# The first experts without two TensorE products, the branch for extra blocks two experts earlier, and y evicted before it is split

## The chip, the cores and the metric

The kernel is one program on one NeuronCore of a Trainium2 chip. Its five engines are TensorE (PE in the profile), VectorE (DVE), ScalarE (ACT), GpSimd (POOL) and SyncE (SP), which here only issues DMAs. The metric is the time of one execution on the device, in microseconds (us), as a median over runs.

## The reference

256 tokens of width 1024 go through a first block (retention, a feed-forward layer, stick-breaking attention, another feed-forward layer) and then through a second block. The change lies wholly in the second block's last part, a mixture of 32 experts in 4 groups: each token takes the best group, and in it the best two experts. Cut to what matters:

```python
g_prob = softmax(xt @ w_rg + b_rg)
g_w, g_idx = top_k(g_prob, 1)                 # the group
e_top, e_loc = top_k(e_logits of that group, 2)
e_w = softmax(e_top) * g_w                    # two weights a token
# every expert e, for the tokens sent to it:
y = (silu(x @ w_gate[e]) * (x @ w_up[e])) @ w_down[e]     # 1024 -> 2 x 512 -> 1024
out[token] += y * e_w
...
x = x + gate2 * ffn                           # gate2: one row of 1024 numbers
return rms_norm(x, g_final)
```

`gate2` is the last of six rows that a small product of `c` with `w_ada` gives. There is no limit on how many tokens an expert takes.

## The kernel before, in words

**Weights.** All weights stream from HBM in loads of 1 MB through a ring of slots, in the order that `plan` writes down, all issued on SP (`Stream.fill`, L132). In the experts the order is four loads of gate and up weights of expert 0 (`gu`), four of expert 1, two of down weights of expert 0 (`dn`), four of expert 2, two of down weights of expert 1, and so on; the last are `gu` 31, `dn` 30, `dn` 31. Before the experts the ring is extended to 21 slots. A load is issued when PE has read the slot that it goes into, so up to 21 loads are ahead of PE.

**Routing.** `last` (L1484 on) ends the norm in front of the experts. For each half of the tokens (t = 0, 1) `choose` finds groups and experts on DVE, `rank` (PE, tile `next`) counts each token's place in its expert, and `first_hot` (DVE, tile `goh`) makes the one-hot matrix that picks the rows of experts 0 and 1. `gather_steps` multiplies it on PE with x (tile `xg`, L1715); `gather_out` brings the result to SBUF with scale and shift. Small `idle` products (L1417) keep PE going between. `position`, `weights` and `route_rest` finish the slots and weights of all tokens, `spread` makes `gate2` in 128 partitions on PE (tile `gate`, L650), and `spread_rows` does the same for positions and weights (tile `rows`, L1651).

**An expert.** An expert has 64 slots, and two experts a pair q = e // 2. `gate_up` is 16 matmuls of 512 columns (two records each in the trace: x32), L1736, then SiLU on ACT and a product on DVE. `h_T` transposes the result on PE (L1748) and DVE copies it (L1757). `down` is 8 matmuls (x16), L1771. `evac` brings each half of y out of PSUM, times weight and gate (DVE, L1888), and splits it into a high part `Yh` (ACT, L364) and a low part `Yl` (DVE, L365). `sc` (L1899) adds a pair's rows to the tokens' sums in PSUM (tile `acc`) by 8 matmuls with a matrix S of slots; the sums have begun with x, put there by 8 products with the identity (`add_x`, L1906). Every two pairs, `gather` (L1694) fetches the rows of the next ones, and `one_hot` makes its matrix on DVE.

**The order of the loop** is written out in `experts`. In turn e: `gate_up(e)`; for odd e, `sc` of the pair before and S of this pair; `dn(e - 1)`, with the transposition of e in its middle; at some e the gather. `overflow` holds the blocks of experts with more than 64 rows. It is a loop under a condition on a count, and every engine reads the count (L1812) and branches by itself (L1813); here the count is 0 and the body does not run. It stands at the end of turn 30, behind `dn(29)`, since it uses ring slots that are free only once all loads have been issued. After the last `sc` come the final norm and four output DMAs.

Of the kernel before, what the change touches and what calls it, by code (L numbers as in the profile page):

```python
# [12 lines left out]
F32 = mybir.dt.float32  # L13
# [8 lines left out]
T = 256  # L22
# [18 lines left out]
I2 = 2  # L41
# [153 lines left out]
class Body:  # L195
# [418 lines left out]
    def ada_steps(self):  # L614
        nc = self.nc
        for s in range(4):
            p = self.w("ada")
            for kc in range(KC):
# [5 lines left out]
                if kc == KC - 1:  # L624
# [3 lines left out]
                    if s == 1:  # L628

                        self.row1 = self.dram.tile([4 * 384], F32, name="row1")  # L630
                        nc.gpsimd.dma_start(out=self.row1.rearrange("(g c) -> g c", g=4), in_=m[0:128:32, :])
# [10 lines left out]

    def spread(self, s, t):

        nc = self.nc
        for i in range(2):
            r = self.w("gate")
            for j in range(4):
                k = 12 * s + 4 + 4 * i + j
                nc.tensor.matmul(r[:, j * 128:j * 128 + 128], self.modc[:, k:k + 1].to_broadcast([128, 128]), self.ident,  # L650
                                 start=True, stop=True)
            nc.scalar.activation(t[:, i * 512:i * 512 + 512], r, AF.Copy)
        return t
# [438 lines left out]
    def mixers(self, xT):  # L1092
# [281 lines left out]
        def gate(_):  # L1374
            self.gate = self.view("gain", [128, D], "gate")
            nc.sync.dma_start(out=self.gate, in_=self.row1[512:1536].partition_broadcast(128))
# [26 lines left out]
    def open_experts(self):  # L1403
# [6 lines left out]
        self.declare(mp, k2=2)  # L1410
        self.st.extend(mp, "ring2", RING2, RING2)
# [36 lines left out]
    def router_norm(self):  # L1448
# [33 lines left out]
        def last():  # L1482
# [29 lines left out]
    def choose(self, t, p, mid=None):  # L1512
# [7 lines left out]
        OH = [rt(f"oh{k}", NT, 32) for k in range(2)]  # L1520
# [21 lines left out]
        V.tensor_scalar(OH[1][:, t, :], io, ei[:, t, 1:2], None, op0=ALU.is_equal)  # L1542
# [11 lines left out]
    def first_hot(self, t, q):  # L1554

        V = self.nc.vector
# [6 lines left out]
    def position(self, t, q):  # L1563
# [3 lines left out]
        lim, tmp, pos = rt("lim", 32), rt("tmp", 32), rt("pos", NT, 2)  # L1567
        V.tensor_tensor(lim, q, self.rc["past"], op=ALU.is_ge)
# [16 lines left out]

    def route_rest(self):
# [5 lines left out]

        se, d, wt = rt("se"), rt("d"), rt("wt", NT, 2)
        V.scalar_tensor_tensor(se, d, 1.0, se, op0=ALU.add, op1=ALU.mult)
        V.reciprocal(wt[:, :, 0], se)
# [6 lines left out]
        for r, src in zip(self.rowsb, (pos, wt)):  # L1602
            yield
            self.spread_rows(r, src)
# [574 lines left out]
```

## Time and profile before

| | |
|---|---|
| three runs | 1367.05, 1364.13, 1362.34 us; median 1364.13 |
| the profiled execution | 1361.64 us, of which the span of its trace is 1359.6 us |
| PE busy | 1323.8 us, 97% of the span |
| DVE, ACT, POOL busy | 867.1, 631.2, 60.1 us |
| moved by DMA | 374.64 MB, at a mean of 276 GB/s |
| the experts | gather from 890.0, first `gate_up` from 896.9, end of the last `dn` 1345.8 us |

Times within the trace count from the span's start. A row of the timeline is a run of like instructions: its start, its length, engine, line, operation, and output and input tiles; in brackets at its end stands how long the engine had been idle before it and which instruction ended the wait. `PEq`, `DVEq` and `SPq` are the engines' sequencers, which hold branches and DMA issues.

### The profile page before, as it was taken

To read this page: it belongs to the slowest core of one execution; us is meant where nothing else is said; L and a number is where in the kernel's file an instruction comes from. 1 tells how busy PE (TensorE), PEld (TensorE's weight loads), DVE (VectorE), ACT (ScalarE), POOL (GpSimd) and SP (SyncE) were. 2 spreads that over 40 slices of the span, in tenths; PEclk is the share of its full clock that TensorE was granted. 3 is DMA by queue.
4 is the path that set the end of the run, shared out by engine and by line. 5 is a ranking of instruction groups with operands and counts; after the bars stand their busy time and mean duration, and the time that the engine had idled before them with its cause. 6 is when DMAs were issued, how large, how long until landed. Compare 5 with 4: busy or idle time off the path is not lost. (4 is left out here: it accounts for less than half of the span.)

```text
span 1359.6 us, 21183 instructions
## 1 busy us (share of the span) xinstructions
PE 1323.8 (97%) x8108; PEld 975.2 (72%) x8108; DVE 867.1 (64%) x1823; ACT 631.2 (46%) x1227; POOL 60.1 (4%) x117
## 2 busy tenths in 40 slices
PE   9999999999999999999999999999999999999986
PEld 7888878999989998999996899864434434344332
DVE  7757757777776666877777778645635544544344
ACT  5554546666667776666666666532212111111112
POOL 0000001000010000000002222100000000000000
PEclk9999999999999999999999999989999999999998
DMA  9755459544447323844446844789999999999994
GB/s 362 303 191 180 132 207 398 198 186 186 155 164 293 115 95 121 356 186 186 185 141 228 368 166 160 276 328 370 420 420 421 420 421 421 420 421 421 421 420 162
DMA packets 56857, 374.64 MB, mean 276 GB/s; under 512 B 7085, under 2 KB 7905, under 8 KB 15666
## 3 DMA queue, kind: packets, MB, share of 16 engines
q1 hardware_dynamic: 55440, 369.66, 69.2%
q0 software_dynamic: 1168, 3.54, 0.8%
q8 instruction: 64, 1.05, 0.3%
q14 instruction: 39, 0.32, 0.1%
q10 hardware_dynamic: 146, 0.07, 0.0%
HBM read 372.19 MB, written 1.05 MB: 275 GB/s over the span
## 5 line engine op out<-in xcount | busy, mean ns | idle before, releaser
L157 DVE TENSOR_TENSOR lo<-ring,hi 128x512 fp32r<-128x512 f32 x519 | 334.9, 687 | 100.5 <-ACT hi L154 94.6
L154 ACT ACTIVATE hi<-ring 128x512 fp32r<-128x512 f32 x519 | 300.6, 623 | 119.8 <-PE nat_ps L360 40.2
L1736 PE MATMUL gu<-ring,x 128*64 128x512 f32 x920 | 207.2, 598 | 15.9 <-DVEq L1813 5.6
L358 PE MATMUL up<-xT,hi 128*128 128x256 f32 x704 | 199.5, 283 | 0.0
L360 PE MATMUL up<-xT,lo 128*128 128x256 f32 x704 | 199.2, 283 | 0.0
L359 PE MATMUL up<-xT,hi 128*128 128x256 f32 x704 | 199.2, 283 | 0.0
L1736 PEld LDWEIGHTS gu<-ring,x 128*64 128x64 f32 x920 | 64.9, 138 | 147.9 <-issue 117.7
L364 ACT ACTIVATE Yh<-y 64x512 fp32r<-64x512 f32 x64 | 40.2, 629 | 213.8 <-DVE y L1888 182.3
L358 PEld LDWEIGHTS up<-xT,hi 128*128 128x128 f32 x704 | 134.0, 190 | 2.0 <-issue 1.2
L359 PEld LDWEIGHTS up<-xT,hi 128*128 128x128 f32 x704 | 134.0, 190 | 0.8
L360 PEld LDWEIGHTS up<-xT,lo 128*128 128x128 f32 x704 | 134.0, 190 | 0.0
L1771 PE MATMUL y<-ring,early 128*64 128x512 f32 x480 | 115.4, 602 | 1.2 <-DMA ring<-dn 0.6
L1740 ACT ACTIVATE h<-gu 64x512 f32<-64x512 f32 x32 | 18.8, 589 | 156.4 <-PE gu L1736 123.5
L813 DVE SCALAR_TENSOR_TENSOR slab<-up,conv,slab 128x254 f32<-128x254 f32 (+1 forms) x176 | 72.7, 476 | 25.7 <-ACT slab L809 25.2
L1741 DVE TENSOR_TENSOR h<-h,gu 64x512 f32<-64x512 f32 x32 | 22.1, 692 | 102.5 <-ACT h L1740 101.8
L365 DVE TENSOR_TENSOR Yl<-y,Yh 64x512 fp32r<-64x512 f32 x64 | 43.9, 686 | 45.7 <-ACT Yh L364 45.7
L358 PE MATMUL nat_ps<-hi,xT 128*128 128x512 f32 x176 | 69.2, 393 | 0.0
L360 PE MATMUL acc<-hi,slab 128*128 128x512 f32 x176 | 69.2, 393 | 0.0
L358 PE MATMUL acc<-hi,slab 128*128 128x512 f32 x176 | 68.9, 391 | 0.0
L359 PE MATMUL acc<-lo,slab 128*128 128x512 f32 x176 | 68.7, 390 | 0.0
L360 PE MATMUL nat_ps<-hi,xT 128*128 128x512 f32 x176 | 68.6, 390 | 0.0
L359 PE MATMUL nat_ps<-lo,xT 128*128 128x512 f32 x176 | 68.6, 390 | 0.0
(450 smaller groups left out, 2509.8 us busy)
## 6 DMA issues: line engine op xcount, KB each, us to landing
ring<-gu SPq DMA_DIRECT2D x123, 1024.0 KB, 19.8
ring<-dn SPq DMA_DIRECT2D x59, 1024.0 KB, 19.8
ring<-ffn_u SPq DMA_DIRECT2D x44, 1024.0 KB, 4.9
ring<-ada SPq DMA_DIRECT2D x32, 768.0 KB, 4.3
ring<-ret_w SPq DMA_DIRECT2D x22, 1024.0 KB, 11.1
ring<-ffn_d SPq DMA_DIRECT2D x22, 1024.0 KB, 4.9
ring<-sb SPq DMA_DIRECT2D x12, 1024.0 KB, 6.3
ring<-ret_o SPq DMA_DIRECT2D x8, 1024.0 KB, 9.2
```

Source lines behind the costliest of these rows:

```text
L154: self.nc.scalar.activation(hi, src, AF.Copy)
L157: (eng or self.nc.vector).tensor_tensor(lo, src, hi.bitcast(F32), op=ALU.subtract)
L358: mm(out, l[0], r[0], start=start, stop=False, **k)
L359: mm(out, l[0], r[1], start=False, stop=False, **k)
L360: mm(out, l[1], r[0], start=False, stop=stop, **k)
L364: self.nc.scalar.activation(hi, src, AF.Copy)
L365: self.nc.vector.tensor_tensor(lo, src, hi.bitcast(F32), op=ALU.subtract)
L813: nc.vector.scalar_tensor_tensor(u[:, c, s:], p[:, c * T:c * T + T - s], cw[:, n - 1 - s:n - s], u[:, c, s:], op0=ALU.mult, op1=ALU.add)
L1736: nc.tensor.matmul(p[64 * i:64 * i + 64, :], xs(kc), raw[:, i * 512:i * 512 + 512], start=kc == 0, stop=kc == KC - 1)
L1740: nc.scalar.activation(h[64:128, :], p[0:64, :], AF.Silu)
L1741: nc.vector.tensor_tensor(h[64:128, :], h[64:128, :], p[64:128, :], op=ALU.mult)
L1771: nc.tensor.matmul(p[64 * i:64 * i + 64, :], hT[:, c, :], raw[:, h * 512:h * 512 + 512], start=c == 0, stop=c == 3)
```

## The change

It has three parts.

- **The first experts.** `gate2` is no longer made on PE. Its row is written to HBM by a DMA on POOL's queue and read back into 128 partitions by a second one, where the ring is extended (512 KB). The sums begin with copies of x into PSUM by ACT (three) and DVE (one), in `seed`, so `add_x` goes. Both `spread_rows` come before expert 1's `gate_up`, not behind it. The first one-hot matrix is made on POOL, the first gather is four steps of four matmuls with the second `rank` behind the first, and no idle products stand between.
- **The branch** (`overflow`) moves from the end of turn 30 to turn 29, behind `gate_up(29)`, `sc(13)`, the load of the final norm's gain and the transposition of 29; that result goes into the free half of the gain's ring slot. `dn(28)` and the gather that stood ahead of it are now behind it.
- **y.** Both halves are evicted, then both are split. `sc` multiplies all high parts first and then all low parts. Seven idle products stand ahead of the last `sc`.

The first place is PE at the start of the experts. Before, from the idle products behind the first `rank` to the first half of `dn(0)` (`next` is a rank, `gate` the spread of gate2, `acc<-x` the sums' beginning):

```order
L1417 MATMUL idle<-ident 128x128 x4
L1715 MATMUL xg<-goh,x 128x128 x8
L1548 MATMUL next<-early 128x32
L1550 MATMUL next<-M,early 128x32
L1551 MATMUL next<-M,early 128x32
L1417 MATMUL idle<-ident 128x128 x2
L1715 MATMUL xg<-goh,x 128x128 x8
L1736 MATMUL gu<-ring,xg 64x512 x16
L650 MATMUL gate<-ident,modc 128x128 x8
L1748 MATMUL hT<-ident,h 128x64 x4
L1906 MATMUL acc<-x,ident 128x512 x4
L1736 MATMUL gu<-ring,xg 64x512 x16
```

And now, over the same stretch up to expert 1's `gate_up`:

```order
L1409 MATMUL idle<-ident 128x128 x4
L1732 MATMUL xg<-goh,x 128x128 x4
L1551 MATMUL next<-early 128x32
L1553 MATMUL next<-M,early 128x32
L1554 MATMUL next<-M,early 128x32
L1732 MATMUL xg<-goh,x 128x128 x12
L1753 MATMUL gu<-ring,xg 64x512 x16
L1668 MATMUL rows<-ident,pos 128x128 x4
L1668 MATMUL rows<-ident,wt 128x128 x4
L1765 MATMUL hT<-ident,h 128x64 x4
L1753 MATMUL gu<-ring,xg 64x512 x16
```

The second `rank` stands four gather products earlier, the `gate` and `acc` products are gone, and the `rows` products, which followed expert 1's `gate_up`, stand ahead of it.

The second place is PE around the branch. Before, it stands behind `dn(29)`:

```order
L1736 MATMUL gu<-ring_12657,x 64x512 x4
L1771 MATMUL y<-ring_12663,early 64x512 x4
L1748 MATMUL hT<-ident,h 128x64 x4
L1771 MATMUL y<-ring,early 64x512 x4
L1812 TENSOR_LOAD tabi
L1813 COMPARE_AND_BRANCH
```

And now behind the transposition of 29, with `dn(28)` still to come:

```order
L1753 MATMUL gu<-ring,x 64x512 x16
L1922 MATMUL acc<-Yh,S 128x512 x4
L1922 MATMUL acc<-Yl,S 128x512 x4
L1765 MATMUL hT<-ident,h 128x64 x4
L1828 TENSOR_LOAD tabi
L1829 COMPARE_AND_BRANCH
```

What PE had done ahead of the branch, `dn(28)`, a gather, `gate_up(30)` and `dn(29)`, now follows it.

The third place is DVE at the end, from the copy of the last transposition on (`y` is the product with weight and gate, `Yl` the low part). Before:

```order
L1757 COPY early<-hT 128x256
L1888 SCALAR_TENSOR_TENSOR y<-y,ws,gate_10392 64x512
L365 TENSOR_TENSOR Yl<-y,Yh 64x512
L1888 SCALAR_TENSOR_TENSOR y<-y,ws,gate_10392 64x512
L365 TENSOR_TENSOR Yl<-y,Yh 64x512
L1888 SCALAR_TENSOR_TENSOR y<-y,ws,gate_10392 64x512
L365 TENSOR_TENSOR Yl<-y,Yh 64x512
```

And now:

```order
L1774 COPY early<-hT 128x256
L1907 SCALAR_TENSOR_TENSOR y<-y,ws,gate_10117 64x512 x2
L367 TENSOR_TENSOR Yl<-y,Yh 64x512 x2
L1907 SCALAR_TENSOR_TENSOR y<-y,ws,gate_10117 64x512 x2
L367 TENSOR_TENSOR Yl<-y,Yh 64x512 x2
```

The product of the second half no longer stands behind the low part of the first.

The diff, cut to its core:

```diff
-I2 = 2
+I2 = 7
+OVER = E - 3
...
-    def spread(self, s, t):                      # gate2 on PE: gone
...
     def open_experts(self):
...
+        self.gate2 = mp.tile([128, D], F32, name="gate2")
+        nc.gpsimd.dma_start(out=self.gate2, in_=self.gates[3][512:1536].partition_broadcast(128))
...
             self.idle(I1)
-            self.choose(1, p, lambda: self.first_hot(0, q0))
-            self.xg0 = self.gather_steps(self.first, 128)
-            next(self.xg0)
+            qs = self.small("q0")
+            nc.scalar.activation(qs, q0[:, 0:2], AF.Copy)
+            self.first_hot(0, qs, nc.gpsimd)
+            self.choose(1, p)
+            xg = self.gather_steps(self.first, 128)
+            next(xg)
             q1 = self.rank(1)
-            self.idle(I2)
+            next(xg)
             self.first_hot(1, q1)
-            self.qs = q0, q1
+            self.weights()
+            self.table("silu")
+            self.sums = [self.seed(0, (nc.scalar, nc.scalar))]
+            for t, q in enumerate((q0, q1)):
+                self.position(t, q)
+            next(xg)
+            self.xg0 = next(xg)
+            self.sums.append(self.seed(1, (nc.vector, nc.scalar)))
+            self.slot_weights()
+            self.split_x()
...
+    def seed(self, t, engs):
+        out = []
+        for h, eng in enumerate(engs):
+            p, x = self.a("acc"), self.x[:, t, h * 512:h * 512 + 512]
+            if eng is self.nc.scalar:
+                eng.activation(p, x, AF.Copy)
+            else:
+                eng.tensor_copy(p, x)
+            out.append(p)
+        return out
...
-        for i in (odd, 1 - odd):
-            r, h = slice(64 * i, 64 * i + 64), i ^ odd
-            evac(i, r, h, p[r, :])
+        rows = [slice(64 * i, 64 * i + 64) for i in (odd, 1 - odd)]
+        evac([(r, h, p[r, :]) for h, r in enumerate(rows)])
...
+            def evac(parts):
+                fs = []
+                for r, h, p in parts:
+                    f = mp.tile([128, 512], F32, tag="k2", name="y", bufs=2)
+                    nc.vector.scalar_tensor_tensor(f[r, :], p, W[e // 2][h][r, :], ...)
+                    fs.append(f)
+                for (r, h, _), f in zip(parts, fs):
+                    self.hilo(hi[r, h, :], lo[r, h, :], f[r, :])
...
-            if e > 1 and odd:
-                sc(q - 1)
+            if odd:
+                if e > 1:
+                    sc(q - 1)
+                if e == OVER:
+                    gain = st.spare()
+                    nc.sync.dma_start(out=gain[:, 0:D], in_=a["g_final"].partition_broadcast(128))
+                    hTs[e] = self.h_T(hs.pop(e), gain[:, D:D + 256].rearrange(...))()
+                    self.overflow(accs)
+                    hot(q + 1)
                 S[q] = slots(self.slot_rows, q)
...
-                dn(e - 1, turn)
...
+                dn(e - 1, turn if e in hs else None)
+            else:
+                self.all_rows()
                 turn()()
-                self.split_x()
-                add_x()
...
-            if e == E - 2:
-                gain = st.spare()
-                nc.sync.dma_start(out=gain[:, 0:D], in_=a["g_final"].partition_broadcast(128))
-                self.overflow(accs)
         dn(E - 1)
+        self.idle(I2)
         sc(E // 2 - 1)
```

## Rows read from the trace of the kernel before

**Rows 1.** Page, parts 1 and 2: busy time; GB/s in 40 slices.

```profile
PE 1323.8 (97%) x8108; PEld 975.2 (72%) x8108; DVE 867.1 (64%) x1823; ACT 631.2 (46%) x1227; POOL 60.1 (4%) x117
...
GB/s 362 303 191 180 132 207 398 198 186 186 155 164 293 115 95 121 356 186 186 185 141 228 368 166 160 276 328 370 420 420 421 420 421 421 420 421 421 421 420 162
```

**Rows 2.** Windows, core 0: engines' busy time, TensorE clock, DMA share, GB/s.

```profile
888.00:890.00 2.00, 2.00 (x10) 2.00 (x11) 1.72 (x11) 0.80 (x5) 0.41 (x2) 0.50 0.99 414
...
896.00:904.00 8.00, 8.00 (x42) 3.07 (x41) 2.83 (x16) 1.50 (x4) 0.00 (x0) 1.00 0.57 179
...
910.00:914.00 4.00, 4.00 (x21) 1.43 (x22) 2.54 (x11) 0.00 (x0) 0.00 (x0) 1.00 0.57 168
...
928.00:936.00 8.00, 7.57 (x36) 2.64 (x38) 1.74 (x4) 1.41 (x4) 0.00 (x0) 1.00 0.66 211
```

**Rows 3.** Timeline of PE from 884 to 931: start, length, group, wait.

```profile
890.02 3.39 PE L1715 MATMUL xg<-goh,x 128*128 128x128 f32 x16
...
894.94 2.05 PE L1715 MATMUL xg<-goh,x 128*128 128x128 f32 x16
...
896.92 7.09 PE L1736 MATMUL gu<-ring,xg 128*64 128x512 f32 x32
...
903.94 2.05 PE L650 MATMUL gate<-ident,modc 128*128 128x128 f32 x16
...
906.31 3.70 PE L1906 MATMUL acc<-x,ident 128*128 128x512 f32 x8
...
909.94 7.09 PE L1736 MATMUL gu<-ring,xg 128*64 128x512 f32 x32
...
916.96 1.16 PE L1651 MATMUL rows<-ident,pos 128*128 128x128 f32 x8
...
918.94 1.94 PE L1771 MATMUL y<-ring,early 128*64 128x512 f32 x8
...
928.43 1.94 PE L1736 MATMUL gu<-ring,x 128*64 128x512 f32 x8 [0.76 <-DVE x L1725]
```

**Rows 4.** Timeline of the SP queue, 895 to 935: weight loads issued.

```profile
898.90 0.33 SPq L132 DMA_DIRECT2D ring<-dn  x1
...
917.07 13.67 SPq L132 DMA_DIRECT2D ring<-gu  x4
```

**Rows 5.** Groups by shape on POOL: busy us, mean ns, idle before.

```profile
L1167 POOL TENSOR_SCALAR G<-mixc 128x129 f32<-128x129 f32 x4 | 2.5, 620 | 32.6 <-DVE sc L1236 13.7 <-DVE mixc L1124 10.4 <-DVE rec L1238 8.5
```

**Rows 6.** Timeline of PE from 1290 to the end.

```profile
1297.55 1.94 PE L1736 MATMUL gu<-ring,x 128*64 128x512 f32 x8 [0.55 <-DMA ring<-gu]
...
1305.58 0.66 PE L1694 MATMUL xg<-goh,xnh 128*128 128x128 f32 x4
...
1310.20 1.94 PE L1736 MATMUL gu<-ring,x 128*64 128x512 f32 x8 [0.84 <-ACT x L1727]
...
1326.91 8.56 PE L1736 MATMUL gu<-ring,x 128*64 128x512 f32 x32 [5.65 <-DVEq L1813]
...
1342.18 3.65 PE L1771 MATMUL y<-ring,early 128*64 128x512 f32 x16 [0.53 <-DVE early L1757]
```

**Rows 7.** Timeline of DVE from 1318 to 1330.

```profile
1325.36 0.68 DVE L365 TENSOR_TENSOR Yl<-y,Yh 64x512 fp32r<-64x512 f32 x1 [0.70 <-ACT Yh L364]
```

**Rows 8.** Chain of waits in order of time, from 1320 to the end.

```profile
1335.48 2.04 PE acc L1899 x8
...
1337.52 1.87 PE y L1771 x8
...
1339.39 0.40 PE hT L1748 x4
...
1346.38 0.69 DVE y L1888
...
1347.09 0.64 ACT Yh L364
...
1349.91 0.68 DVE Yl L365
```

More of the change, by code (lines that the diff above doesn't have):

```diff
@@ L641, in ada_columns @@
                               q[:, 0:384].rearrange("p (j g r) -> p g j r", j=3, r=32)[:, :, :, 0])
-    def spread(self, s, t):
[L645 to L653, printed above, removed]
     def setup(self):
@@ L1519, in choose @@
         gi, ei = rt("gi", NT, 1), rt("ei", NT, 2)
-        OH = [rt(f"oh{k}", NT, 32) for k in range(2)]
+        OH = [rt("oh0", NT, 32)]
         M, pen = rt("M", NT, 32), rt("pen", NT, 4)
@@ L1584, in weights, with slot_weights, all_rows @@
         nc.scalar.activation(d, d, AF.Exp)
+    def slot_weights(self):
+        V, rt = self.nc.vector, self.rt
+        se, d, wt = rt("se"), rt("d"), rt("wt", NT, 2)
+        V.scalar_tensor_tensor(se, d, 1.0, se, op0=ALU.add, op1=ALU.mult)
+        V.reciprocal(wt[:, :, 0], se)
+        V.tensor_tensor(wt[:, :, 1], wt[:, :, 0], d, op=ALU.mult)
+    def all_rows(self):
+        b = self.view("gain", [128, 2, 2 * T], "rows")
+        self.rowsb = [b[:, i, :] for i in range(2)]
+        for r, src in zip(self.rowsb, (self.rt("pos"), self.rt("wt"))):
+            self.spread_rows(r, src)
+    def seed(self, t, engs):
[8 more added lines that the diff above has]
+        return out
     def route_rest(self):
@@ L1895, in sc @@
             ys, ss = Y.pop(p), S.pop(p)
-            for t in range(NT):
-                for j in range(2):
-                    for i, y in enumerate(ys):
-                        nc.tensor.matmul(accs[t][j], ss[j][:, t * 128:t * 128 + 128], y[:, j, :], start=False,
-                                         stop=p == E // 2 - 1 and i == 1, skip_group_check=True)
-        def add_x():
-            for t in range(NT):
-                for j in range(2):
-                    nc.tensor.matmul(accs[t][j], self.ident, self.x[:, t, j * 512:j * 512 + 512], start=True,
-                                     stop=False, skip_group_check=True)
-        self.weights()
-        self.table("silu")
-        xg[0] = next(self.xg0)
-        for t in range(NT):
-            self.position(t, self.qs[t])
+            last = p == E // 2 - 1
+            for i, y in enumerate(ys):
+                for a, b in itertools.product(range(2), range(2)):
+                    t, j = (a, b) if i else (b, a)
+                    nc.tensor.matmul(accs[t][j], ss[j][:, t * 128:t * 128 + 128], y[:, j, :], start=False,
+                                     stop=last and i == 1, skip_group_check=True)
+        accs, xg[0] = self.sums, self.xg0
         rest = self.route_rest()
-        accs = self.accs()
         for e in range(E):
             q, odd, last = e // 2, e % 2, e == E - 1
-            if e > 1 and odd:
+            if odd:
                 W[q] = slots(self.slot_weight, q)
             turns = odd and not last and last_of[q] == q
-            if turns:
+            if turns and e != OVER:
                 hot(q + 1)
@@ L1933, in turn @@
                 return then
-            if e > 1 and odd:
-                sc(q - 1)
+            if odd:
+                if e > 1:
[3 more added lines that the diff above has]
+                    nc.sync.dma_start(out=gain[:, 0:D], in_=a["g_final"].partition_broadcast(128))
+                    hTs[e] = self.h_T(hs.pop(e), gain[:, D:D + 256].rearrange("p (j s) -> p j s", j=4))()
+                    self.overflow(accs)
+                    hot(q + 1)
                 S[q] = slots(self.slot_rows, q)
-            if e == 1:
-                next(rest)
-                next(rest)
-                W[0], S[0] = slots(self.slot_weight, 0), slots(self.slot_rows, 0)
             if e:
-                dn(e - 1, turn)
-            for _ in range(0 if e else 2):
-                next(rest)
-            if not e:
+                dn(e - 1, turn if e in hs else None)
+            else:
+                self.all_rows()
                 turn()()
-                self.split_x()
-                add_x()
             if turns:
```

44 lines of the change are left out of this document (15 added, 29 removed).

## The prediction

> **What bounds the kernel now.** I read the page's busy times and its 40 slices first, then windows over the experts, then the timelines of PE, of the SP queue and of DVE at the two ends of the experts, and the chain of waits last. PE is called busy for 97% of the span, which says little; the row of GB/s says more [rows 1]. From its 29th slice, about 950 us, to the last but one it stands at 420 to 421, level, whatever the experts do: there the loads are at their rate, one of 1.049 MB every 2.49 us (1.049 MB / 421 GB/s), and a PE that needs less than that waits for each one, as at 1297.55, where it had stood 0.55 us for a load [rows 6]. So in the middle of the experts nothing that PE, DVE or ACT saves can count. What counts is the two ends: how soon the loads reach that rate for good, and how much PE has left once they no longer hold it up.
>
> At the entry the loads stop three times, since all 21 slots are full and PE has not yet read the next one. Between 896 and 904 they run at 179 GB/s, between 910 and 914 at 168, between 928 and 936 at 211 [rows 2]. Against 421 that loses 8 x (1 - 179/421) = 4.6 us, 4 x (1 - 168/421) = 2.4 and 8 x (1 - 211/421) = 4.0, 11.0 in all. The last stop ends when PE has read the first slot of expert 2: its matmuls start at 928.43 and take 1.94 [rows 3], and the load issued at 917.07 + 13.67 - 0.33 = 930.41 is the one that waited for them [rows 4]. From there on the loads set the pace to the end, so the end comes as much earlier as expert 2 starts earlier, up to the point where the loads no longer stop.
>
> At the other end PE is last held up by a load at 1297.55. Behind that load stand 16 more (`dn` 28, `gu` 30, `dn` 29, `gu` 31, `dn` 30, `dn` 31), so the last lands at 1297.55 + 16 x 2.49 = 1337.4. PE's last `dn` ends at 1342.18 + 3.65 = 1345.83 [rows 6], 8.4 us later: here PE is the bound, and it lost 5.65 us at the branch (until 1326.91) and 8.56 - 7.09 = 1.47 in the slow matmuls behind it [rows 3, 6].
>
> **The change part by part: the entry.** Of PE's work between the first gather and expert 2, the `gate` products (2.05 us) and the `acc` products with x (3.70, less 0.07 of overlap, by the next row's start) go: 5.7 us [rows 3]. The `rows` products (918.94 - 916.96 = 1.98 us) only move ahead of expert 1, where they stand beside SiLU and the product that the transposition of expert 0 waits for, so that costs nothing; without that cover it would give back its 2.0. The second `rank` and the idle products cost 894.94 - 893.41 = 1.5 us between the two halves of the gather (890.02 + 3.39 and 894.94); now the rank stands between gather products and DVE's one-hot is made beside them, of which I take back 0.6 (0 to 1). The wait of 0.76 ahead of expert 2 goes in part, since ACT and DVE now take one half each of the wide gather: 0.7 with the small gaps (0 to 1). Sum for the start of expert 2: 5.7 + 0.6 + 0.7 = 7.0 us earlier.
>
> How much of this the loads can use follows from the stops: the first can shrink only by the 0.6 that expert 0 starts earlier, the second and third go whole, 0.6 + 2.4 + 4.0 = 7.0. The two ways agree. I take 6.5, since the copies of x and the splits now stand on ACT and DVE in a stretch where I cannot see them; both are far from full there (2.83 and 1.50 of 8 us [rows 2]). The new load of gate2 is 512 KB, half a load, 1.25 us of the loads' time, issued while the ring still fills ahead of the first stop, which hides it; without that cover it costs 1.25. Bounds for the entry: 3 (only the `acc` products count) to 8.5 (all pieces at their upper ends).
>
> The one-hot matrix of the first tokens on POOL has no row. The nearest are four TENSOR_SCALAR of 128x129 on POOL at 620 ns [rows 5]; two of half that width and a small one lie between 0.6 and 1.9, I take 0.9. It replaces 0.8 us of DVE, in front of a first gather that starts at 890.02 and has idle products ahead of it: 0, with -0.5 to +1.0 as bounds. The Trainium skill speaks against it ("SBUF — State Buffer", section on SBUF's two separate sides): GpSimd and VectorE share a pair of ports, exclusively for a whole instruction, and the other is blocked. No run here shows that; by it DVE's chain for the second tokens ends up to 0.9 us later, which still lies beside four gather products, so the sum stays.
>
> **The branch.** At turn 29 PE comes to it from a stretch in which loads hold it up, with the work that now follows it still ahead. Reckoned from the load at 1297.55: last matmuls of `gu` 29, 1.9; `sc` 2.04; transposition 0.40 [rows 6, 8], 1301.9. Then DVE's copy, the branch and PE's restart. Before, the low part on DVE ended at 1325.36 + 0.68 = 1326.04 and PE went on at 1326.91, 0.87 later [rows 6, 7]; with 0.4 for the copy and 0.2 for hand-overs that is 1.5, so 1303.4. Then `dn(28)` 3.7; the gather with its wait, 1310.20 - 1305.58 = 4.6; `gu(30)` 7.0; `dn(29)` 1.87 + 0.40 + 1.89 = 4.2; `gu(31)` 7.0; `sc` 2.0; `dn(30)` 4.2; `dn(31)` 3.6: 1339.7 [rows 3, 6, 8]. That is 6.1 before 1345.83. The loads allow no more than 0.4 beyond: the last one at 1337.4, and 1.9 for the matmuls that read it, 1339.3. Queued behind the branch on DVE are the one-hot matrix for the gather and S, on ACT the splits of `dn(28)`; they run beside `dn(28)`. If the one-hot came late, the gather would wait for at most four operations of DVE of no more than the 0.68 of a 512-wide one [rows 7], 2.7. Bounds of the term: 3.5 to 6.5.
>
> **y at the end.** Before, from the last matmul at 1345.83 to the last low part at 1349.91 + 0.68 = 1350.59 pass 4.76 us, each half in turn through DVE, ACT, DVE. Now DVE makes both products (0.69 + 0.75), while ACT makes the first high part beside the second product; then DVE's first low part and ACT's second high part run together, and the second low part follows (0.68 + 0.68): 2.9 with hand-overs [rows 8]. Gain 1.9 (1 to 2.2; the idle products fit into PE's wait). Earlier pairs have the same change, but there loads set the pace.
>
> Sum: 6.5 + 6.1 + 1.9 = 14.5. Against the profiled execution's 1361.64 that is 1347.1; it lies 2.5 under the median of the runs, 1364.13, against which the same sum gives 1349.6, and I state 1349.5.
>
> **The rivals.** *Only the tail.* ACT and DVE get copies, splits, two `rows` copies and S of the first pair into one short stretch; if one of them holds up expert 1 or the first `dn`, the loads stop as before. Against: their 2.83 and 1.50 of 8 us. Time: 1364.1 - 8.0 = 1356.
>
> *Only entry and y.* The branch stops PE as long at turn 29 as at turn 30, because its length (5.65) lay in the engines' branching and not in the wait for DVE's evictions. For: each engine loads the count. Against: the 0.87 from DVE's end to PE's start. Then 1364.1 - 6.5 - 1.9 = 1355.7.
>
> *Half clock in expert 0.* The granted clock was 0.50 between 888 and 890, that is 1.2 of 2.4 GHz, with PE busy throughout [rows 2], and it had risen for expert 0's 7.09 us. With the idle products between gone and waits in their place, it might rise only behind expert 0, which would then take 14.2: the entry is 7.1 later, 0.6 behind the old one, and the end 1364.1 + 0.6 - 8.0 = 1356.7. The Trainium skill ("TensorE: Matmul & The Clock Gate", What's actually happening) has the slow clock as the default and activity as what releases it; the trace agrees in so far as the level rose after the gather.
>
> *A load behind the branch, slower.* DVE's copy at turn 29 goes into the ring slot whose other half takes the gain, and all loads up to the last, and then the gain, are issued at once. If the copy, or the branch, waits for them, PE stands until the gain has landed at 1338.7 (1337.4 + 1.25) and goes on at 1340; from there 1339.7 - 1303.4 = 36.3 us follow, end 1376.5, 30.7 later than before; with 6.5 and 1.9 taken off, 1386.4. It decides once PE restarts after 1303.4 + 6.1 + 8.4 = 1317.9. Against: the two halves of the slot do not overlap, and the counts that DVE, ACT and PE wait for there are of loads long read.
>
> *No net change.* The entry's gain lost and the branch as long as before, 1362 with y alone.
>
> **How the numbers follow.** Forecast 0.61 (own range 1345 to 1354: entry 3 to 8.5, branch 3.5 to 6.5, y 1 to 2.2, not all at one end). Only the tail 0.13; only entry and y 0.12; half clock 0.05; the slower case 0.04; no net change 0.05. The range reaches over the three cases at 1356 to 1357 and is 1344 to 1359, with about 0.15 outside. A measurement of this kernel tells 0.3%, 4.1 us, from no change, so faster means under 1360.0: the first four cases, 0.91, of which 0.01 is taken off for several losses together; within it 0.06; slower 0.04.
>
> **What would show it.** Expert 2's first matmul 6 to 7.5 us nearer to the start of the first gather, and one stop of the loads, not three, between 896 and 940. At the new branch, PE idle of 1 to 2 us behind DVE's branch, at full clock after it, and PE held up by no load from there on except the last ones. From the end of `dn(31)` to the last low part 2.9 us. It is wrong if `gu(1)` or the first `dn` shows a new wait for ACT or DVE, if PE's stop at the branch stays near 5 us or `dn(28)` waits for a load, or if expert 0 takes over 10 us.

## The result, and the profile after

The changed kernel took 1349.8 us (median of 4 runs, 1348.91 to 1352.98) against 1364.62 (4 runs, 1362.34 to 1367.05): the ratio is 0.9895, with a 95% interval of 0.9871 to 0.992, so 11 to 18 us less. The profiled execution took 1349.12 us with a span of 1347.3, 12.3 less than the span before.

The busy times and the GB/s in 40 slices of the changed kernel:

```profile
PE 1317.9 (98%) x8094; PEld 971.3 (72%) x8094; DVE 867.2 (64%) x1821; ACT 631.8 (47%) x1229; POOL 62.7 (5%) x122
...
GB/s 363 307 193 180 125 195 398 219 181 187 161 173 298 110 102 101 351 188 186 186 149 183 398 180 128 268 338 411 421 421 421 420 421 421 421 421 422 420 418 253
```

The two rows look like those of before [rows 1]; the 28th slice now stands at 411 GB/s and not at 370, so the loads reach their rate a little sooner. The windows over the entry, with the columns of [rows 2], show it plainly:

```profile
896.00:904.00 8.00, 8.00 (x37) 4.01 (x38) 5.10 (x12) 4.59 (x9) 0.00 (x0) 0.83 0.49 169
912.00:916.00 4.00, 4.00 (x20) 1.29 (x18) 1.03 (x4) 0.59 (x1) 0.00 (x0) 1.00 0.98 334
928.00:936.00 8.00, 8.00 (x42) 2.92 (x40) 2.73 (x5) 1.32 (x3) 0.00 (x0) 1.00 1.01 420
```

One stop is left between 896 and 904 (169 GB/s, clock 0.83), and a short one at 912 (334); the third, 211 GB/s between 928 and 936, is gone. Against 421 GB/s the two lose 8 x (1 - 169/421) + 4 x (1 - 334/421) = 5.6 us where the three lost 11.0, so 5.4 less. PE's timeline at the entry, which answers to [rows 3]:

```profile
889.42 2.08 PE L1732 MATMUL xg<-goh,x 128*128 128x128 f32 x8 [0.41 <-POOL goh L1563]
...
892.86 5.47 PE L1732 MATMUL xg<-goh,x 128*128 128x128 f32 x24
898.26 7.28 PE L1753 MATMUL gu<-ring,xg 128*64 128x512 f32 x32
...
907.84 7.09 PE L1753 MATMUL gu<-ring,xg 128*64 128x512 f32 x32
...
922.76 1.94 PE L1753 MATMUL gu<-ring,x 128*64 128x512 f32 x8
```

The gather's last 24 records take 5.47 us and expert 0 starts at 898.26, 1.34 later than before. From there to expert 2 pass 24.5 us where 31.5 passed, so expert 2 is 5.67 earlier. PE at the end, for [rows 6]:

```profile
1292.28 1.94 PE L1753 MATMUL gu<-ring,x 128*64 128x512 f32 x8 [0.55 <-DMA ring<-gu]
...
1298.62 3.65 PE L1788 MATMUL y<-ring,early 128*64 128x512 f32 x16 [1.97 <-DVEq L1829]
...
1322.59 1.94 PE L1753 MATMUL gu<-ring,x 128*64 128x512 f32 x8 [0.45 <-SPq L1829]
...
1331.22 3.65 PE L1788 MATMUL y<-ring,early 128*64 128x512 f32 x16 [0.53 <-DVE early L1774]
```

The last load that comes late ahead of the branch is used 5.27 us earlier, PE stands 1.97 at the branch (5.65 before), and once more, at 1322.59, 0.45 ahead of the matmuls on the last load of `gu` 31. (The trace names SP's branch as what ended this wait; that it was the load is argued from `no_if` below, where there is no branch and the same place waits 0.55 for the load.) From the matmuls of 1292.28 to the end of `dn(31)`, 1331.22 + 3.65 = 1334.87, pass 42.59 us; before it was 48.28. DVE at the end, for [rows 7, 8]:

```profile
1334.92 1.53 DVE L1907 SCALAR_TENSOR_TENSOR y<-y,ws,gate 64x512 f32<-64x512 f32 x2 [0.88 <-PE y L1788]
1336.49 1.40 DVE L367 TENSOR_TENSOR Yl<-y,Yh 64x512 fp32r<-64x512 f32 x2
```

Both products run together, then both low parts; the last one ends at 1337.89, 3.02 behind `dn(31)` where it was 4.76. So the 12.3 us of the two spans come from the entry (5.3), from PE's work behind the last late load (5.7) and from y (1.7), less 0.4 behind the last low part, at the output, which was not followed up.

### The profile page after: what moved, and what is told of

It is laid out like the page before. It is cut to its first block, busy times and chain, and to the rows that moved or that the text cites. A ratio compares the mean times of both kernels' runs of the same rounds, so it can differ in the third digit from the quotient of the medians.

```text
span 1347.3 us, 21166 instructions
## 1 busy us (share of the span) xinstructions
PE 1317.9 (98%) x8094; PEld 971.3 (72%) x8094; DVE 867.2 (64%) x1821; ACT 631.8 (47%) x1229; POOL 62.7 (5%) x122
## 5 line engine op out<-in xcount | busy, mean ns | idle before, releaser
L1788 PE MATMUL y<-ring,early 128*64 128x512 f32 x464 | 111.4, 602 | 3.9 <-DVEq L1829 2.0
L1788 PEld LDWEIGHTS y<-ring,early 128*64 128x64 f32 x464 | 29.7, 136 | 53.3 <-issue 47.4
```

What stands on the lines that cost most here:

```text
L1788: nc.tensor.matmul(p[64 * i:64 * i + 64, :], hT[:, c, :], raw[:, h * 512:h * 512 + 512], start=c == 0, stop=c == 3)
```

## The experiments

All runs below were timed in three sessions; the kernel before stood at 1363.04 us in that of u_branch, u_evac, u_entry and clk, at 1362.92 in that of again, u_two, no_if and warm, and at 1365.0 in that of first, mid, u_pool and best. The table has five points of PE's timeline and one of DVE's from the one profiled execution of each kernel. "Mix" is the end of the last matmul ahead of the router, which the change doesn't touch; "gu 29" is the start of the matmuls on the last load of expert 29. In brackets stands what passed since the point to its left (for the last column, since the end of `dn(31)`); for "end of dn(31)" it is counted from gu 29.

| kernel | median, us | ratio to before (95%) | mix | expert 0 | expert 2 | gu 29 | end of dn(31) | last low part |
|---|---|---|---|---|---|---|---|---|
| before | | 1 | 882.4 | 896.92 (+14.5) | 928.43 (+31.5) | 1297.55 | 1345.83 (+48.3) | +4.76 |
| changed | 1349.8 | 0.9895 (0.9871 to 0.992) | 882.5 | 898.26 (+15.8) | 922.76 (+24.5) | 1292.28 | 1334.87 (+42.6) | +3.02 |
| again | 1350.43 | 0.991 (0.9894 to 0.9925) | 883.1 | 897.68 (+14.5) | 922.00 (+24.3) | 1291.12 | 1334.70 (+43.6) | +3.03 |
| u_branch | 1353.68 | 0.993 (0.9914 to 0.9945) | 883.8 | 898.24 (+14.5) | 922.58 (+24.3) | 1292.22 | 1338.85 (+46.6) | +3.01 |
| u_evac | 1353.82 | 0.993 (0.9915 to 0.9945) | 883.4 | 895.04 (+11.7) | 920.53 (+25.5) | 1289.30 | 1333.48 (+44.2) | +4.76 |
| u_entry | 1354.88 | 0.9932 (0.9917 to 0.9947) | 884.0 | 897.89 (+13.9) | 928.09 (+30.2) | 1297.38 | 1340.85 (+43.5) | +3.01 |
| u_two | 1355.8 | 0.9949 (0.9936 to 0.9963) | 883.7 | 898.50 (+14.8) | 928.23 (+29.7) | 1297.73 | 1339.85 (+42.1) | +3.02 |
| first | 1354.51 | 0.9926 (0.9911 to 0.994) | 883.4 | 897.96 (+14.5) | 927.38 (+29.4) | 1297.34 | 1340.40 (+43.1) | +3.02 |
| mid | 1349.71 | 0.9886 (0.9867 to 0.9905) | 886.2 | 900.86 (+14.6) | 925.21 (+24.4) | 1295.51 | 1339.14 (+43.6) | +3.01 |
| no_if | 1349.22 | 0.9899 (0.9884 to 0.9915) | 883.5 | 898.23 (+14.8) | 922.57 (+24.3) | 1292.06 | 1334.39 (+42.3) | +3.01 |
| u_pool | 1350.62 | 0.9894 (0.9878 to 0.9909) | 885.7 | 900.40 (+14.7) | 924.75 (+24.4) | 1293.84 | 1337.05 (+43.2) | +3.01 |
| clk | 1349.84 | 0.99 (0.9881 to 0.9918) | 882.6 | 897.75 (+15.2) | 922.10 (+24.4) | 1291.84 | 1335.45 (+43.6) | +3.03 |
| warm | 1348.78 | 0.9893 (0.9877 to 0.9908) | 887.1 | 899.35 (+12.2) | 923.66 (+24.3) | 1294.59 | 1338.21 (+43.6) | +3.02 |
| best | 1348.95 | 0.9884 (0.9866 to 0.9902) | 886.2 | 898.47 (+12.2) | 922.82 (+24.4) | 1292.93 | 1337.50 (+44.6) | +3.01 |

In all rows gu 29 lies 368.8 to 370.9 us behind expert 2: what expert 2 gains at the entry arrives there.

**u_branch: the branch back to turn 30.**

```diff
-                if e == OVER:
-                    gain = st.spare()
-                    ...
-                    self.overflow(accs)
...
+            if e == E - 2:
+                gain = st.spare()
+                ...
+                self.overflow(accs)
```

It is one turn of the loop later, not the two experts of the title.

> The changed kernel with the branch alone put back behind dn(29), at the end of turn 30. Theory (PE pays for the branch only where no load holds it up): from the start of the matmuls on the last load of gu 29 to the end of dn(31) 48 us again, as before (48.3), against 42.6 in the changed kernel; the whole 5.7 us slower, 1355.5, ratio to before 0.993. PE idle at the branch 5 to 6 us, less the share that the earlier low parts take off. Rival (the branch itself is cheap and the changed kernel won by the clock behind it alone): 1.5 us slower, 1351.3.

PE at the branch and at the last `dn`:

```profile
1292.22 1.94 PE L1753 MATMUL gu<-ring,x 128*64 128x512 f32 x8 [0.54 <-DMA ring<-gu]
...
1319.72 8.78 PE L1753 MATMUL gu<-ring,x 128*64 128x512 f32 x32 [4.66 <-DVEq L1829]
...
1335.20 3.65 PE L1788 MATMUL y<-ring,early 128*64 128x512 f32 x16 [0.53 <-DVE early L1774]
```

The ratio is 0.993, about 3.7 us above the two timings of the changed kernel (uncertain by some 2.7), less than forecast. From the last late load to the end of `dn(31)` pass 46.6 us, 3.0 to 4.0 more than in the changed kernel's two traces, and 1.7 fewer than before: with the new order of y PE stands 4.66 at the old branch and not 5.65, and the gather ahead of expert 30 no longer waits 0.84 for ACT.

**u_evac: y as before.**

```diff
-        rows = [slice(64 * i, 64 * i + 64) for i in (odd, 1 - odd)]
-        evac([(r, h, p[r, :]) for h, r in enumerate(rows)])
+        for i in (odd, 1 - odd):
+            r, h = slice(64 * i, 64 * i + 64), i ^ odd
+            evac([(r, h, p[r, :])])
...
-            for i, y in enumerate(ys):
-                for a, b in itertools.product(range(2), range(2)):
-                    t, j = (a, b) if i else (b, a)
+            for t, j in itertools.product(range(2), range(2)):
+                for i, y in enumerate(ys):
                     nc.tensor.matmul(accs[t][j], ...)
...
-        self.idle(I2)
         sc(E // 2 - 1)
```

> The changed kernel with the halves of y evicted and split one after the other, the old order in sc, and no idle products ahead of the last sc. Theory (only the last pair counts, since loads set the pace before it): 4.8 us from the end of dn(31) to the last low part against 3.0, 1.7 slower, 1351.5; the last load of gu 29 lands at the same time within 0.5 us. Rival (all pairs count): 16 pairs with 0.5 to 1 us each, 8 us or more slower. Second rival (the order in sc hides it): no difference, 1349.8.

The first experts in this trace, and the first load of expert 30:

```profile
890.30 1.16 PE L1732 MATMUL xg<-goh,x 128*128 128x128 f32 x8 [0.62 <-POOL goh L1563]
...
892.19 2.92 PE L1732 MATMUL xg<-goh,x 128*128 128x128 f32 x24
895.04 7.09 PE L1753 MATMUL gu<-ring,xg 128*64 128x512 f32 x32
...
1305.19 1.94 PE L1753 MATMUL gu<-ring,x 128*64 128x512 f32 x8 [0.47 <-ACT x L1744]
```

This takes back three pieces at once (the order of products and splits, the order in `sc`, the seven idle products); what each is worth was not run. The end is as forecast, 4.76 us from `dn(31)` to the last low part. The whole is 0.993, 3.7 us above the changed kernel, more than the 1.7; by the intervals this difference is uncertain by some 2.7. The gather ahead of expert 30 waits 0.47 for ACT again, so the order of y counts in the other evictions behind the last late load, too. And this execution shows something that was not looked for: the same first experts as in the changed kernel, with the granted clock at 1.00 throughout. The gather's last 24 records take 2.92 us and not 5.47, and expert 0 starts 11.7 behind the mix. Its time, 1349.47, is the lowest of this kernel's six by 3.5 us.

**u_entry: the first experts as before.** The kernel before with the other two parts put in (their lines are those of the diff above).

> The kernel before with the other two parts of the change (branch at turn 29, both halves of y evicted first) and its own first experts. Theory: three stops of the loads again, the last load of gu 29 used at 1297.5 as before and not at 1292.3; then 42.6 us to the end of dn(31) as in the changed kernel; 5.3 us slower than the changed kernel, 1355.1, ratio to before 0.993. Rival (what the entry gives is lost again later, and the changed kernel's gain lies in the tail alone): 1350.

PE at the last late load and behind the branch:

```profile
1297.38 1.94 PE L1737 MATMUL gu<-ring,x 128*64 128x512 f32 x8 [0.55 <-DMA ring<-gu]
...
1303.70 5.21 PE L1772 MATMUL y<-ring,early 128*64 128x512 f32 x16 [1.94 <-DVEq L1813]
```

As forecast: 1354.88, and the last late load at 1297.38 (1297.55 before). By the spans of the traces it is 5.6 us above the changed kernel (1352.9 against 1347.3), by the ratios 3.0 to 5.0. Within this noise the entry's gain reaches the end whole.

**clk: the second rank behind the first tokens' gather.**

```diff
-I1 = 4
+I1 = 7
...
             next(xg)
-            q1 = self.rank(1)
             next(xg)
+            q1 = self.rank(1)
+            self.idle(2)
             self.first_hot(1, q1)
```

> The changed kernel with seven idle products instead of four behind the first rank, the second rank behind both gather products of the first tokens, and two idle products behind that rank. Theory (the first gather ran at half clock until 898.3 because the short products of the second rank and a gap of 0.41 us stand in it): the granted clock is back at 1.00 by 893 to 894, the gather's 32 matmuls take 5.5 us and not 7.6, expert 0 starts at 896.5 to 897 instead of 898.26, and the end comes as much earlier: 1.3 to 1.8 us, 1348.2. Rival (expert 0's start is set by ACT or DVE, or the later rank costs what the clock gives): expert 0 at 898 or later, 1349.8 or more.

PE at the entry:

```profile
891.43 2.81 PE L1733 MATMUL xg<-goh,x 128*128 128x128 f32 x16
...
895.77 2.05 PE L1733 MATMUL xg<-goh,x 128*128 128x128 f32 x16
897.75 7.09 PE L1754 MATMUL gu<-ring,xg 128*64 128x512 f32 x32
```

The clock was back at 0.89 between 893 and 894, as forecast, but it had also fallen earlier, between 886 and 887, and expert 0 starts at 897.75, 15.2 behind the mix. The time is the changed kernel's. One trace at another place of the fall can't show what the order of the rank is worth; this is left open.

**again: the changed kernel once more.**

> The changed kernel once more, unedited, for a second trace. In the traces with its first experts so far expert 0 started at 898.2 (two of them) and at 895.0 (one, in which the granted clock did not fall in the first gather), and dn(28) behind the branch took 3.65 in one and 5.2 to 5.4 at half clock in three. Theory (where the clock falls differs from execution to execution of the same program, and this makes most of its spread): the median is 1349 to 1351 again, and at least one of the two places differs by over 1 us from the first trace. Rival (the place is fixed by the program): expert 0 at 898.3 and dn(28) 3.65 again.

PE in this second trace, at the entry and behind the branch:

```profile
893.53 4.22 PE L1732 MATMUL xg<-goh,x 128*128 128x128 f32 x24
897.68 7.09 PE L1753 MATMUL gu<-ring,xg 128*64 128x512 f32 x32
...
1297.46 3.65 PE L1788 MATMUL y<-ring,early 128*64 128x512 f32 x16 [1.98 <-DVEq L1829]
...
1319.92 1.94 PE L1753 MATMUL gu<-ring,x 128*64 128x512 f32 x8 [0.56 <-DMA ring<-gu]
1322.41 1.94 PE L1753 MATMUL gu<-ring,x 128*64 128x512 f32 x8 [0.56 <-SPq L1829]
```

The same program, and the gather's last records take 4.22 us and not 5.47. `dn(28)` runs at full clock, 3.65, in both traces; it does so too in u_two, first and u_pool, and takes 5.2 to 5.4 in u_evac, u_entry, clk, warm and mid at half clock. Behind the branch two loads now hold PE up (0.56 each), which is why this trace has 43.6 to `dn(31)`'s end with a quick `dn(28)`: the last load of `gu` 31 is used 31.3 us behind that of `gu` 29, 30.3 in the first trace, and 12 loads of 2.49 us are 29.9. Why these loads came 1.4 us late is open.

**u_two: gate2 and the sums' beginning on PE again.**

```diff
-        nc.gpsimd.dma_start(out=self.gate2, in_=self.gates[3][512:1536].partition_broadcast(128))
...
-            self.sums = [self.seed(0, (nc.scalar, nc.scalar))]
...
+                self.spread(3, self.gate2)
                 self.all_rows()
                 turn()()
+                add_x()
```

> The changed kernel with gate2 spread on PE again and the sums begun by products of x with the identity, all else of the entry as changed. Theory (the start of expert 2 is PE's sum, and the loads follow it): expert 2 starts 5.5 us later than in the changed kernel at a like start of expert 0, one more stop of the loads shows, and the end is 5 us later: 1355, as with the whole entry put back (1354.9). Rival (the order of the rows products, of the gather and the POOL one-hot carry the entry's gain): under 2 us later, 1351.5.

PE at the entry:

```profile
898.50 7.09 PE L1762 MATMUL gu<-ring,xg 128*64 128x512 f32 x32
905.51 2.05 PE L652 MATMUL gate<-ident,modc 128*128 128x128 f32 x16
...
909.67 3.70 PE L1940 MATMUL acc<-x,ident 128*128 128x512 f32 x8
...
928.23 1.94 PE L1762 MATMUL gu<-ring,x 128*64 128x512 f32 x8
```

As forecast: 29.7 us from expert 0 to expert 2 and not 24.4, and 1355.8 us against 1350.43 in the same session, 5.4 more. The two products of 2.05 and 3.70 us are the entry's gain.

**mid and first: 22 idle products at two places.** The same edit at expert 12 and at expert 1:

```diff
+            if e == 12:        # first: e == 1
+                self.idle(22)
             hs[e] = self.gate_up(...)
```

> The changed kernel with 22 idle products (5.7 us by the 0.26 of each of the seven ahead of the last sc) ahead of expert 12's gate and up matmuls. Theory (between the stops at the entry and the last experts the loads set the pace and hold several slots ahead of PE): PE is 5.7 us later at expert 12 and not at all at the last load of gu 29; no difference, 1350. Rival (PE, called busy for 97% of the span, is the bound there): 5.7 us slower, 1355.8.

> The changed kernel with the same 22 idle products ahead of expert 1's gate and up matmuls. Theory (what delays the first use of slots at the entry delays every later load): expert 2 starts 5.7 us later, the loads stop again, the last load of gu 29 is used 5.2 to 5.7 later, 1355.5. Rival (the lead of the ring takes it up as in the middle): 1350 to 1351.

PE in mid, at expert 12 and at the first wait for a load:

```profile
1053.68 5.18 PE L1409 MATMUL idle<-ident 128*128 128x128 f32 x44
...
1220.49 1.94 PE L1753 MATMUL gu<-ring,x 128*64 128x512 f32 x8 [0.55 <-DMA ring<-gu]
```

The products take 5.18 us. At expert 12 they cost nothing: 1349.71, and gu 29 lies 370.3 us behind expert 2, within the spread of the other kernels. At expert 1 they cost 4.8 us against mid: 1354.51; expert 2 starts 29.4 and not 24.4 us behind expert 0, and all later loads follow. The first wait for a load stands at 1220 here, at 1237 in the trace before and at 1170 in the changed kernel's: until then, as it seems, PE works off the lead of the ring. A delay larger than that lead was not tried.

**warm: four idle products ahead of the second logits.**

```diff
-I1 = 4
+I1 = 7
...
+            self.idle(4)
             p = logits(1)
```

> The changed kernel with four idle products more ahead of the logits of the second tokens, and seven instead of four behind the first rank. Theory (the clock falls because of the stretch of short products of 36 and 32 columns ahead of the first gather, and dense products within it hold it up in most executions): granted clock 1.00 from 885 to 898, expert 0 at 895.5 to 896, 0.5 later than in the trace in which the clock did not fall and 2.5 earlier than where it fell; median 1347.5. Rival (it falls all the same): the four products cost 0.5 to 0.9, median 1350.5.

Windows of this kernel, with the columns of [rows 2]:

```profile
888.00:892.00 4.00, 4.00 (x39) 4.00 (x38) 3.08 (x18) 3.14 (x6) 0.00 (x0) 1.00 1.01 389
892.00:896.00 4.00, 4.00 (x31) 3.63 (x30) 2.68 (x16) 1.34 (x7) 1.82 (x5) 1.00 1.02 426
```

And the same windows of the changed kernel's first trace:

```profile
888.00:892.00 4.00, 3.59 (x19) 3.00 (x17) 2.00 (x11) 2.38 (x8) 1.52 (x4) 0.56 1.01 414
892.00:896.00 4.00, 4.00 (x20) 4.00 (x20) 2.21 (x16) 0.93 (x2) 0.00 (x0) 0.50 1.01 422
```

The clock stays at 1.00 where it was 0.56 and 0.50, and expert 0 starts 12.2 us behind the mix, not the 14.5 to 15.8 of the traces in which it fell. It fell in six of the seven traces with the changed kernel's own entry and in neither of the two with these products (warm and best), so that they hold it up is likely and not shown. In its traced execution the mix itself ended 4.6 us late, of which the last section tells. The median, 1348.78, is 1.65 below the changed kernel's in the same session; the intervals overlap, so that it is faster is likely and not shown.

**no_if: no branch at all.** `overflow` ends behind its two `spare` slots; the reading of the count, the branch and the blocks for experts with more than 64 rows are left out, which this input doesn't need.

> The changed kernel without the condition and the loop for extra blocks (left out: what experts with more than 64 rows would need; there are none in this input). Theory (at turn 29 the branch is nearly hidden, since the last loads allow no more): from the start of the matmuls on the last load of gu 29 to the end of dn(31) 41.7 at the least (16 loads of 2.49 and 1.9) against 42.6 to 44.2, so 0.9 to 2 us faster, 1348.3. Rival (the branch still costs its wait and the half clock behind it): 3.5 us faster, 1346.3.

PE from where the branch was:

```profile
1296.38 3.65 PE L1788 MATMUL y<-ring,early 128*64 128x512 f32 x16
...
1319.59 1.94 PE L1753 MATMUL gu<-ring,x 128*64 128x512 f32 x8 [0.74 <-DMA ring<-gu]
1322.08 1.94 PE L1753 MATMUL gu<-ring,x 128*64 128x512 f32 x8 [0.55 <-DMA ring<-gu]
```

PE goes on at 1296.38, 4.3 us behind the start of `gu` 29's last matmuls and not 6.3, and then waits for loads: 0.74 and 0.55 ahead of the last two of `gu` 31. To the end of `dn(31)` pass 42.3 us, 0.3 and 1.3 less than in the changed kernel's two traces. 1349.22 against 1350.43 in the session, with overlapping intervals: the branch is nearly hidden where it stands now.

**u_pool: the first one-hot matrix on DVE.**

```diff
-            self.first_hot(0, qs, nc.gpsimd)
-            self.choose(1, p)
+            self.choose(1, p, lambda: self.first_hot(0, q0))
```

> The changed kernel with the first one-hot matrix made by DVE inside the second choose, as before, and not by POOL. Theory (where it is made is worth under 1 us, since in the traces with POOL DVE's chain for the second tokens took 2.77 us beside it and 2.70 without it): the first gather product 6.9 to 7.6 us behind the last product of the mix, as with POOL, median within 1 us of the changed kernel, 1349.5 to 1351. Rival (POOL and DVE block each other, so that DVE alone is quicker): 1349 or less, expert 0 1 us earlier at a like clock.

1350.62, and the first gather product 6.8 us behind the mix, against 7.0 in both traces of the changed kernel: no difference that can be told. In the changed kernel POOL makes the matrix in this stretch of its timeline:

```profile
887.48 0.28 POOL L1561 TENSOR_SCALAR first<-M,rx 128x2 f32<-128x2 f32 x1 [14.06 <-DVE M L1545]
888.20 1.16 POOL L1563 TENSOR_SCALAR goh<-early,q,first 128x64 f32<-128x64 f32 x2 [0.44 <-POOL first L1561]
```

And these are the first and the last operation of DVE's two chains, with one between them that has two inputs:

```profile
884.66 0.22 DVE L1530 SCALAR_TENSOR_TENSOR gp<-logits,rx,early 128x4 f32<-128x4 f32 x1 [0.64 <-PE logits L1471]
...
885.87 0.20 DVE L1539 TENSOR_TENSOR eb<-eb,pen 128x32 f32<-128x32 f32 x1
...
887.11 0.25 DVE L1545 SCALAR_TENSOR_TENSOR M<-early,ei,oh 128x32 f32<-128x32 f32 x1
887.28 0.22 DVE L1530 SCALAR_TENSOR_TENSOR gp<-logits,rx,early 128x4 f32<-128x4 f32 x1
...
888.51 0.19 DVE L1539 TENSOR_TENSOR eb<-eb,pen 128x32 f32<-128x32 f32 x1
...
889.80 0.25 DVE L1545 SCALAR_TENSOR_TENSOR M<-early,ei,oh 128x32 f32<-128x32 f32 x1
```

DVE's chain for the first tokens takes 887.36 - 884.66 = 2.70 us, and the one for the second, beside POOL's 1.44, 890.05 - 887.28 = 2.77, without the reciprocal of 0.16 that stands in the first; so some 0.2 may be lost beside POOL. The Trainium skill ("SBUF — State Buffer", section on SBUF's two separate sides) would have the one blocked for the whole of the other's instruction, where DVE's runs in a two-port mode or reads two SBUF inputs while POOL's reads SBUF. These operations don't show that: `eb<-eb,pen`, with its two inputs, took 0.19 us beside POOL's `goh` and 0.20 in the first chain.

**best: idle products behind the branch, too.** The kernel of warm with this besides:

```diff
                     self.overflow(accs)
+                    self.idle(4)
                     hot(q + 1)
```

> The kernel with four idle products more ahead of the second logits and seven behind the first rank, and besides four idle products right behind the branch, so that PE has work while it would wait for DVE there. Theory (two places at which the clock falls in most executions are covered): expert 0 at 12 us behind the last product of the mix instead of 14.5, dn(28) at 3.65 us and not 5.3; median 1347.5, at most 2 us better than the changed kernel, since from the last load of gu 29 on the loads allow no less than 41.7. Rival (the clock falls by what lies before, and the products only add their own time): 1350.5.

PE behind the branch:

```profile
1299.35 2.05 PE L1409 MATMUL idle<-ident 128*128 128x128 f32 x8 [2.02 <-DVEq L1830]
1301.33 4.24 PE L1789 MATMUL y<-ring,early 128*64 128x512 f32 x16
```

The idle products wait for DVE's branch like everything else behind it (2.02 us), run at half clock and add 2.05 us; `dn(28)` still takes 4.24. That half of the theory is wrong. The other half held: expert 0 at 12.2 us again. 1348.95, as warm without them: neither separates from the changed kernel.

## Why the prediction was right

It said 1349.5 and 14.5 us less; measured are 1349.8 and 14.8 by the medians, 12.3 by the two spans. Where the time is lost and what gives it back was right. That the medians agree to 0.3 is in part luck: the three terms, 14.5 together, come to 5.3 + 5.7 + 1.7 = 12.7 in the first trace and to 6.4 + 4.7 + 1.7 = 12.8 in the second, and the second timing of the changed kernel is 12.5 below that of the kernel before in its session. The terms were not quite what they were called, either.

- **The entry, 6.5 forecast, 5.3 measured (6.4 in the second trace).** Its core was right: u_two shows the two PE products to be worth 5.4 us, first shows that a delay here reaches the end, and the time from expert 0 to expert 2 fell by 7.0 (forecast 6.4). The step that failed is "of which I take back 0.6" for the order of the rank and the idle products: expert 0 came 1.34 later in the first trace, since the granted clock was 0.50 from 889 to 898 and the gather's 24 records took 5.47 us. So the first stop of the loads, which was to shrink by 0.6, did not shrink (4.8 us against 4.6), and 0.8 of the second is left. The fall of the clock was the mechanism of the rival *half clock in expert 0*, one step earlier and at under half of its price; I had put 0.05 on it. u_evac's trace, with the same entry at full clock, shows the price: expert 0 3.2 us earlier and the last late load 3.0. The kernel before had lost the clock there, too, from 886 to 893; it rose within the first half of the gather, not after the gather, so the rows from which the 0.6 was taken are in part at half clock.
- **The branch, 6.1 forecast.** The distance to the end of `dn(31)` fell by 5.7 and, in the second trace, by 4.7. But u_branch gives the move only 3.0 to 4.0 of it. The other 1.7 are the new order of y, which shortens the stop at the old branch and ends the gather's wait for ACT. I priced y at the last pair alone, "there loads set the pace", and forgot the pairs behind the last late load. The stop that is left is 1.97 where I had 1.5 for the copy, the branch and the restart: before, DVE's sequencer read the count (0.55 us from 1325.9) beside the last low part, and now it reads it (0.54 from 1297.3) behind the copy, which ends at 1297.11, so 1.51 and not 0.87 pass from DVE's end to PE's start. The floor by the loads, 41.7 from the last load of all, was set a little low: it is the last load of `gu` 31 that holds PE, 12 x 2.49 = 29.9 us on, and 1334.87 - 1322.59 = 12.3 us of work follow it, 42.2 in all. no_if, without any branch, gets to 42.3, u_two to 42.1.
- **y, 1.9 forecast.** At the end 1.74. With the share above, u_evac's trace gives 2.4 (48.9 from the last late load to the last low part, against 46.5 to 46.6 in u_entry, clk, warm and mid, which have the same slow `dn(28)`); its timing says 3.7, uncertain by 2.7. Whether more than 2.4 is real stays open.
- **The slower rival** is refuted: DVE copied the transposition at 1296.69, while SP issued the last load at 1315 and the gain at 1317.62; the copy waited for neither.
- **"A PE that needs less than that waits for each one"** is wrong for most of the stretch from 950 on. The loads are at their rate there, but PE first waits for one at 1237 in the trace before. What I drew from it, that nothing saved there counts, is borne out by mid, in which 5.2 us lost there did not count.

## What to carry to other kernels

A stream of loads that runs at its rate to the end makes, as here, only two stretches worth work: the one before it first runs without a stop, and the one behind the last load that comes late. Ask of each edit how much of it lies in one of the two, and count every place in it that has the same pattern, not just the last. Where the profile shows half clock in a short stretch of small matmuls, take its price into the range before trusting a trace: the same program shows it in one execution and not in the next.

## What the runs showed of the hardware

The granted clock falls at different places in different executions of one program. In the first gather it was 0.50 from 889 to 898 in one execution of the changed kernel, from 890 to 896 in the second, and it did not fall at all in u_evac, which has the same instructions there. The Trainium skill ("TensorE: Matmul & The Clock Gate", What's actually happening) says of the rise of the clock at a kernel's start that its moment varies from run to run of one kernel. These traces agree, and show it of a fall in the middle, too.

The clock goes with the spread of the times. Of the kernel before's eleven executions in the session of mid, those with a mean granted clock of 0.992 took 1361.4 to 1363.1 us, those with 0.990 took 1364.1 to 1366.5, and those with 0.987 and 0.988 took 1366.2 and 1367.5.

One trace can lie far from another ahead of anything that was changed. In mid, best, u_pool and warm the mix ends at 885.7 to 887.1, in the ten others at 882.4 to 884.0. A part of this comes from one place. The window of the changed kernel's first trace there:

```profile
500.00:540.00 40.00, 39.64 (x238) 35.21 (x238) 22.92 (x39) 25.85 (x45) 0.00 (x0) 1.00 0.32 115
```

And that of warm's:

```profile
500.00:540.00 40.00, 39.63 (x228) 35.13 (x227) 21.28 (x33) 23.51 (x39) 0.00 (x0) 0.91 0.26 93
```

At 0.91 instead of 1.00 over 40 us PE would lose 3.6 us there; between DVE's operations on both sides of the stretch 3.1 us more pass in warm. In mid, best and u_pool the clock is 0.96 there and 1.6 us more pass. The other 1.5 to 2.2 us by which these four lie behind the changed kernel's first trace are there 40 us into the span already, and have two sources. The first product of `q` starts at 12.06 to 12.70 and not at 11.42; in mid ACT stands 1.32 us for a load of `x` ahead of it. And the next of these products (128x256) take 0.41 us each until 14.5 to 15.4, where the changed kernel's take 0.28 from 12.28 on. These four executions took 1351.2 to 1353.4 us, the other executions of mid, warm and best 1347.9 to 1350.5, those of u_pool 1349.6 to 1351.2. So the profile of one execution can lie up to 5 us from another's before it comes to the change, and of two traces one compares distances between points of the same stretch, as the table does, before the spans.
